# A two-layer diffusion backbone on one core: layer 1's modulation vectors formed on DVE during the dense layer instead of on TensorE in layer 0's scan

## The chip, the cores and the metric

The kernel runs on one core of a Trainium2 chip. The metric is the device time of one execution in microseconds; the median of three runs is given, and one more execution was taken with the hardware profiler.

## The reference, cut to what matters

Two layers work on 256 context tokens and 256 latent tokens of width 1024. Each layer first forms six modulation vectors of 1024 numbers for each of two conditioning vectors, `c` (latent tokens) and `c_ctx` (context tokens):

```python
def modulation(cond, w, b):
    return jnp.split(jax.nn.silu(cond) @ w + b, 6, axis=-1)

h = rms_norm(x, gains[0]) * (1.0 + m[1]) + m[0]        # into the mixers
x = x + m[2] * rms_norm(y, gains[1])                   # behind the output projection
h = rms_norm(x, gains[2]) * (1.0 + m[4]) + m[3]        # into the channel mixer
x = x + m[5] * rms_norm(f, gains[3])
```

The matrix `mod_w[l]` is 1024 x 6144 in float32, 25 MB for a layer. Layer 0 uses all six vectors for both conditioning vectors. Layer 1 drops its context tokens behind the mixers, so for `c_ctx` it uses only the first two. Between the modulated norm and the output projection each layer runs four groups of heads (a bidirectional RWKV-7 recurrence and three kinds of attention). Layer 0's channel mixer is a dense SwiGLU of inner width 2816, layer 1's a mixture of eight experts.

## The kernel before

**Products.** A large product is made of three float32r matmuls (`mm3`): each operand is split into a high and a low part. For weights, a chunk `wr` is loaded by SP's queue (1 MB), ScalarE (ACT) writes the high part `wh`, and VectorE (DVE) the low part `wl` (`wsplit`, lines 189 and 194). Raw chunks and split chunks have three slots each in layer 0's later part.

**Modulation.** `mod_round(l, r)` forms two of the six vectors, a third of a layer's modulation: 16 loads of 128 x 1024 by SP's queue into the four `mw` slots of the pool `mp`, 32 float32 matmuls on TensorE (line 324) with the conditioning vectors `sC` as the stationary operand, padded to 32 columns; then a copy `ms` out of PSUM, four transposes and two additions of the bias into `modT[l]`. The four column pieces of a round go to four groups of 32 rows of one PSUM bank.

**Order.** Instructions are put on the engines by a scheduler that takes what is ready by its own reckoning, in order of priority, which is program order; each engine then runs its queue in that fixed order. A tile whose address was that of an earlier pool waits until the earlier pool is released. Round (0, 0) runs at the start. The rounds (0, 1), (0, 2), (1, 0), (1, 1) and (1, 2) stand in the program behind layer 0's scan, and the scheduler fits their matmuls into what it takes for gaps in the attention, the scan and its readout.

**Layer 0 around the change.** The RWKV recurrence is done as a chunked scan: four chunks of 128 tokens, two directions, a chain of small matmuls with DVE, ACT and POOL between them (`stage_a` to `state`; POOL's subtraction into `R` is line 822, the last matmuls are those of line 875). Then `modS.close()` gives back `mp` and its PSUM bank, and the pools of the output projection are opened, on the same side of SBUF: three raw weight slots first. The readout of the scan (normalisation and gate, lines 979 to 1017) writes `yT[0:2]` and their high and low parts `yh`, `yl`; the other six parts of `yT` come from the attention. The output projection multiplies `yT[2:8]` with weight chunks 0 to 2 and `yT[0:2]` with chunk 3, first for two blocks of 128 tokens, and after a normed addition to the reloaded stream `X` for the other two. `X` is loaded again where `yT` is given back.

**The dense layer.** `ffn` goes through ten chunks of 256 inner columns in five groups of two, and an eleventh by itself. A chunk's gate and up products take all four PSUM banks `mm`; `swiglu` makes `sg` (two slots), `ah` and `al` out of them; behind each second chunk two passes of down products (`ch`) follow, in the four banks `dn`, whose results DVE adds to `fo`. `fg` (two slots) and `xn` (three) are used for norms ahead of and behind this loop. POOL makes the low parts `hl` of the layer's input (line 402).

Of the kernel before, what the change touches and what calls it, by code (L numbers as in the profile page):

```python
# [9 lines left out]
F32 = mybir.dt.float32  # L10
# [4 lines left out]
ALU = mybir.AluOpType  # L15
# [3 lines left out]
D = 1024  # L19
# [133 lines left out]
def kernel(ctx, tc, I, out, dbg=None, stop=None):  # L153
    nc = tc.nc
    dbg = dbg or {}
    V, S_, G, T, SP = nc.vector, nc.scalar, nc.gpsimd, nc.tensor, nc.sync

    cpool = ctx.enter_context(tc.tile_pool(name="cpool", bufs=1))
# [69 lines left out]
    ident = cc("ident")  # L228
    ccol = cpool.tile([128, 16], F32, name="ccol")
    prmt = cpool.tile([128, 2, NPR], F32, name="prmt")  # L230
    prm = [prmt[:, 0], prmt[:, 1]]
# [70 lines left out]
    sC = mp.tile([128, 8, 32], F32, name="sC")  # L302
    V.memset(sC, 0.0)
    sg = cpool.tile([128, 16], F32, name="sg")
    S_.activation(sg, ccol, AF.Tanh, scale=0.5)
    V.tensor_scalar(sg, sg, 0.5, 0.5, op0=ALU.mult, op1=ALU.add)
    for i in range(2):
        V.tensor_tensor(sC[:, :, i], sg[:, 8 * i:8 * i + 8], ccol[:, 8 * i:8 * i + 8], op=ALU.mult)


    modT = [cpool.tile([128, 2, 48], F32, tag="modT", name=f"modT{l}", bufs=2) for l in range(2)]

    def mod_round(l, r):
        pm = mps.tile([128, 512], F32, tag="mod", name="pm", bufs=1)
        for k in range(8):
            for jh in range(2):
                w = mp.tile([128, 1024], F32, tag="mw", name="mw", bufs=4)
                c0 = r * 2048 + jh * 1024
                d = SP.dma_start(out=w, in_=I["mod_w"][l, k * 128:k * 128 + 128, c0:c0 + 1024])
                if l == 0 and r == 0:  # L320
                    WP["first"] = ordered(d)
                for j2 in range(2):
                    j = 2 * jh + j2
                    T.matmul(pm[32 * j:32 * j + 32, :], sC[:, k, :], w[:, j2 * 512:j2 * 512 + 512],  # L324
                             start=(k == 0), stop=(k == 7))
        ms = mp.tile([128, 512], F32, tag="ms", name="ms", bufs=1)
        V.tensor_copy(ms, pm)
        pt = mps.tile([128, 512], F32, tag="mod", name="pt", bufs=1)
        for s in range(4):
            T.transpose(pt[:, s * 128:s * 128 + 128], ms[:, s * 128:s * 128 + 128], ident)  # L330
        pv = pt.rearrange("p (s j c) -> p c j s", s=4, j=4)
        for i in range(2):
            V.tensor_tensor(
                modT[l][:, i, 16 * r:16 * r + 16].rearrange("p (j s) -> p j s", j=4), pv[:, i],
                prm[l][:, 16 * r:16 * r + 16].rearrange("p (j s) -> p j s", j=4), op=ALU.add)

    def scales(l, sec, gi):

# [34 lines left out]
    H = {}  # L373
# [34 lines left out]
    def xn_tile(pool):  # L408
        return pool.tile([128, D + 4], F32, tag="xn", name="xn", bufs=3)
# [161 lines left out]
    def rwkv_mix(l, L, sxa, Sx, rsw, sm, gq, ml, nq, nk_, nv, yT, need):  # L571
# [8 lines left out]
        ps = open_ps(kS, f"pt{l}")  # L580
# [11 lines left out]
        for tb in range(4):  # L592
            p = ps("ra", 1)
# [18 lines left out]
        for q in range(2):  # L612
            p = ps("ra", 1)
# [10 lines left out]
        ps = open_ps(fS, f"rp{l}")  # L624
# [11 lines left out]
        for d in range(2):  # L636
            order = ORD[d]
            first, last = (0, 127) if d == 0 else (127, 0)
            for q in range(2):
# [4 lines left out]
                for a in range(2):  # L644
                    p = ps("rw", 6)
                    for j in range(2):
                        T.matmul(p[:, j * 256:j * 256 + 256],
                                 lw[:, 2 * a + j, d * 256 + q * 128:d * 256 + q * 128 + 128], cc(f"tri{d}"),
                                 start=True, stop=True)
                    pv = p.rearrange("p (j c) -> p j c", j=2)  # L650
# [3 lines left out]
                for n in range(3):  # L654
                    V.tensor_tensor(gg[:, n:n + 1], ee[:, order[n], 128 + last:129 + last],
                                    hm[:, order[n + 1]:order[n + 1] + 1], op=ALU.mult)
                p = ps("rw", 6)
                T.matmul(p, wu[64:128, 512 + d * 256 + q * 128:512 + d * 256 + q * 128 + 128], Sx[6][64:128],
                         start=True, stop=True)
# [27 lines left out]
        for a in range(2):  # L687
            p = ps("rw", 6)
# [259 lines left out]
            while run:  # L948
                run = [g for g in run if next(g, run) is None]
        if l == 0:  # L950
            for m in ((0, 1), (0, 2), (1, 0), (1, 1), (1, 2)):
                mod_round(*m)
        qS.close()
        rBS.close()
# [11 lines left out]
        pm, ht = H["p"], H["t"]  # L966
# [3 lines left out]
        ps = open_ps(oS, f"op{l}")  # L970
# [8 lines left out]
        for q in range(2):  # L979
            p = ps("rw", rwb)  # L980
# [9 lines left out]
        for i in range(4):  # L990
            d, q = i // 2, i % 2
            p = ps("rw", rwb)
# [10 lines left out]
        for i in range(4):  # L1003
            p = ps("rw", rwb)
# [310 lines left out]
    def ffn(l):  # L1315
        sk = ExitStack()
        fp = sk.enter_context(tc.tile_pool(name="ffn", bufs=1))
        ps, pd = H["p"], H["q"]
        fo = fp.tile([128, 4, D], F32, name="fo")
        hh, hl = H["h"]  # L1320
        A2, B2 = scales(l, 4, 2), modT[l][:, :, 24:32]
        hT_half(0, A2, B2, ps, "mm")
        ap_ = sk.enter_context(tc.tile_pool(name="fa", bufs=1))

        def products(g, u, bank, parts):

            if bank is None:
                bank = [[ps("mm", 4) for _ in range(2)] for _ in range(2)]
            for a, b in parts:
                for w, pp in zip((g, u), bank):  # L1330
                    for j in range(2):
                        js = slice(j * 128, j * 128 + 128)
                        for k in range(8):
                            mm3(pp[j][:, a:b], w[0][:, k, js], w[1][:, k, js], hh[:, k, a:b], hl[:, k, a:b],
                                k == 0, k == 7)
            return bank

        def swiglu(bank, ah, al, t, a, b):

            for j, (pg, pu) in enumerate(zip(*bank)):  # L1340
                sg = ap_.tile([128, 512], F32, tag="sg", name="sg", bufs=2)
                S_.activation(sg[:, a:b], pg[:, a:b], AF.Silu)
                V.tensor_tensor(sg[:, a:b], sg[:, a:b], pu[:, a:b], op=ALU.mult)
                S_.activation(ah[:, t + j, a:b], sg[:, a:b], AF.Copy)
                V.tensor_tensor(al[:, t + j, a:b], sg[:, a:b], ah[:, t + j, a:b].bitcast(F32), op=ALU.subtract)


        W = [(wtile(I["fgate"][0], 8), wtile(I["fup"][0], 8))]
        bank = products(*W[0], [[pd("dn", 4) for _ in range(2)] for _ in range(2)], ((0, 256),))
        with tc.high_priority(offset=400):  # L1350
            hT_half(1, A2, B2, ps, "mm")
        products(*W[0], bank, ((256, 512),))
        groups = [(c, c + 2) for c in range(0, 10, 2)]
        for gi, (c0, c1) in enumerate(groups):
            nt = 2 * (c1 - c0)
            ah = ap_.tile([128, 4, 512], F32R, tag="ah", name="ah")
            al = ap_.tile([128, 4, 512], F32R, tag="al", name="al")
            for c in range(c0, c1):
                if c:
                    g, u = wtile(I["fgate"][c], 8), wtile(I["fup"][c], 8)  # L1360
                    bank = products(g, u, None, ((0, 512),))
                swiglu(bank, ah, al, 2 * (c - c0), 0, 512)
            f0 = 2 * c0
            for ch in range(2):
                cs = slice(ch * 512, ch * 512 + 512)
                pts = [pd("dn", 4) for _ in range(4)]
                for t in range(0, nt, 4):
                    m = min(4, nt - t)
                    w = wtile(I["fdown"][ch, :, (f0 + t) * 512:(f0 + t + m) * 512], m)
                    for tb in range(4):  # L1370
                        ts = slice(tb * 128, tb * 128 + 128)
                        for k in range(m):
                            mm3(pts[tb], ah[:, t + k, ts], al[:, t + k, ts], w[0][:, k], w[1][:, k],
                                t + k == 0, t + k == nt - 1)
                for tb in range(4):
                    if gi == 0:
                        act_copy(fo[:, tb, cs], pts[tb])
                    else:
                        V.tensor_tensor(fo[:, tb, cs], fo[:, tb, cs], pts[tb], op=ALU.add)

        gb = [gate_bc(fp, ps, "mm", 4, l, 5, 3, i) for i in (1, 0)]
        ah = ap_.tile([128, 4, 512], F32R, tag="ah", name="ah")
        al = ap_.tile([128, 4, 512], F32R, tag="al", name="al")
        g, u, w = wtile(I["fgate"][10], 8), wtile(I["fup"][10], 8), wtile(I["flast"], 2)
        for a in range(0, 4, 2):
            bank = products(g, u, None, ((a * 128, a * 128 + 256),))
            swiglu(bank, ah, al, 0, a * 128, a * 128 + 256)
            for tb in (a, a + 1):
                ts = slice(tb * 128, tb * 128 + 128)
                for ch in range(2):  # L1390
                    cs = slice(ch * 512, ch * 512 + 512)
                    p = pd("dn", 4)
                    for k in range(2):
                        mm3(p, ah[:, k, ts], al[:, k, ts], w[0][:, k, cs], w[1][:, k, cs], k == 0, k == 1)
                    V.tensor_tensor(fo[:, tb, cs], fo[:, tb, cs], p, op=ALU.add)
            add_normed(H["t"], lambda j, c: fo[:, a + j, c * 512:c * 512 + 512], lambda j: ap_.tile([128, D], F32, tag="fg", name="fg", bufs=2), a,
                       gb[a // 2])
        sk.close()
# [269 lines left out]
```

## Time and profile before

| | before |
|---|---|
| median of 3 runs | 2147.05 us (2142.52 to 2150.84) |
| the profiled execution | 2151.0 us, its span 2149.2 us |
| mean granted TensorE clock | 0.970 |
| TensorE busy (PE) | 2017.5 us, 94% |
| VectorE busy (DVE) | 1348.6 us, 63% |
| ScalarE busy (ACT) | 1118.2 us, 52% |
| GpSimd busy (POOL) | 135.2 us, 6% |

The span is the time from the first to the last instruction of the profiled execution. Times of the trace count from its start. A matmul of float32 operands shows as two records in the trace, one of float32r operands as one. The granted clock is the share of TensorE's full clock (2.4 GHz) that was granted in a stretch. "x" stands ahead of the number of instructions, and an arrow stands ahead of what ended a wait.

### The profile page before, as it was taken

What the parts mean: (1) busy time and instruction counts of PE and PEld (TensorE: products, weight loads), DVE (VectorE), ACT (ScalarE), POOL (GpSimd) and SP (SyncE); (2) the same over time, 40 slices, a digit from 0 to 9 for tenths busy, and PEclk for the clock granted to TensorE, in tenths of its full rate; (3) what the DMA queues carried; (4) which work ended last, traced back from release to release, by engine and by line L of the source; (5) the groups of instructions that cost most, each with busy time, mean ns of one, the idle gap of its engine ahead of it and who ended that gap; (6) DMA issues with size and microseconds to landing.
All of it is one profiled execution on the core that took longest, in us unless ns stands there. A gap on an engine that the chain in (4) does not pass through costs nothing. (4 is left out here: it accounts for less than half of the span.)

```text
span 2149.2 us, 28380 instructions
## 1 busy us (share of the span) xinstructions
PE 2017.5 (94%) x11290; PEld 1547.2 (72%) x11290; DVE 1348.6 (63%) x1934; ACT 1118.2 (52%) x1511; POOL 135.2 (6%) x159
## 2 busy tenths in 40 slices
PE   5999989997999999989997887999999999999997
PEld 2985446743788888879745876878787878787775
DVE  2354475433633333475556556888888888888887
ACT  3344653431532222253464455777676767677774
POOL 1100030120100000011002114000000000000000
PEclk8999999997999999999998998999999999999998
DMA  8411123456222222233001033998899989898993
GB/s 305 149 59 40 59 99 138 139 188 262 79 98 98 98 93 91 85 127 110 1 1 60 2 122 129 354 355 337 330 361 341 345 333 362 340 346 329 351 354 137
DMA packets 65005, 408.62 MB, mean 190 GB/s; under 512 B 7328, under 2 KB 7584, under 8 KB 22880
## 3 DMA queue, kind: packets, MB, share of 16 engines
q1 hardware_dynamic: 62480, 397.69, 49.7%
q0 software_dynamic: 992, 4.92, 0.7%
q10 hardware_dynamic: 1392, 4.11, 0.5%
q8 instruction: 91, 1.49, 0.3%
q14 instruction: 50, 0.41, 0.1%
HBM read 404.60 MB, written 2.10 MB: 189 GB/s over the span
## 5 line engine op out<-in xcount | busy, mean ns | idle before, releaser
L194 DVE TENSOR_TENSOR wl<-wr,wh 128x2048 fp32r<-128x2048 f32 (+3 forms) x395 | 749.6, 1909 | 289.4 <-ACT wh L189 288.4
L189 ACT ACTIVATE wh<-wr 128x2048 fp32r<-128x2048 f32 x327 | 623.3, 1909 | 268.2 <-PE mm L277 91.4
L277 PE MATMUL mm<-wl,gh 128*128 128x512 f32 x704 | 280.4, 398 | 5.5 <-DVE wl L194 5.0
L276 PE MATMUL mm<-wh,gh 128*128 128x512 f32 x704 | 284.5, 404 | 0.4 <-DVE sg L1583 0.4
L278 PE MATMUL mm<-wh,gl 128*128 128x512 f32 x704 | 278.4, 395 | 0.0
L276 PE MATMUL mm<-hh,wh 128*128 128x512 f32 (+1 forms) x544 | 200.9, 369 | 0.8 <-ACT gbc L281 0.8
L278 PE MATMUL mm<-hh,wl 128*128 128x512 f32 (+1 forms) x544 | 200.7, 369 | 0.0
L277 PE MATMUL mm<-hl,wh 128*128 128x512 f32 (+1 forms) x544 | 200.6, 369 | 0.0
L277 PEld LDWEIGHTS mm<-wl,gh 128*128 128x128 f32 x704 | 132.5, 188 | 39.0 <-DVE wl L194 12.1
L278 PEld LDWEIGHTS mm<-wh,gl 128*128 128x128 f32 x704 | 132.3, 188 | 30.6
L276 PEld LDWEIGHTS mm<-wh,gh 128*128 128x128 f32 x704 | 132.3, 188 | 29.2 <-DVE sg L1583 0.5
L278 PE MATMUL yd<-wh,al 128*128 128x512 f32 x352 | 139.7, 397 | 0.0
L277 PE MATMUL yd<-wl,ah 128*128 128x512 f32 x352 | 139.6, 397 | 0.0
L276 PE MATMUL yd<-wh,ah 128*128 128x512 f32 x352 | 130.2, 394 | 0.0
L324 PE MATMUL pm<-mw,sC 128*32 128x512 f32 x384 | 94.4, 677 | 28.3 <-DMA mw<-in_mod_w_dram 21.2
L276 PE MATMUL mm<-wh,hh 128*128 128x256 f32 (+2 forms) x352 | 108.4, 311 | 10.8 <-ACT wh L189 9.4
L276 PEld LDWEIGHTS mm<-hh,wh 128*128 128x128 f32 x544 | 102.6, 189 | 18.2 <-ACT gbc L281 1.0
L278 PEld LDWEIGHTS mm<-hh,wl 128*128 128x128 f32 x544 | 102.5, 188 | 17.3
L277 PEld LDWEIGHTS mm<-hl,wh 128*128 128x128 f32 x544 | 102.6, 189 | 17.2
L278 PE MATMUL mm<-wh,hl 128*128 128x256 f32 (+2 forms) x352 | 108.1, 310 | 1.4 <-POOL hl L402 1.2
L277 PE MATMUL mm<-wl,hh 128*128 128x256 f32 (+2 forms) x352 | 108.3, 309 | 0.0
L281 ACT ACTIVATE ah<-tr 128x256 fp32r<-128x256 f32 x88 | 33.6, 382 | 105.3 <-PE tr L1559 105.3
(415 smaller groups left out, 3249.3 us busy)
## 6 DMA issues: line engine op xcount, KB each, us to landing
wr<-in_mgu_dram SPq DMA_DIRECT2D x176, 1024.0 KB, 5.5
wr<-in_mdown_dram SPq DMA_DIRECT2D x88, 1024.0 KB, 5.0
mw<-in_mod_w_dram SPq DMA_DIRECT2D x96, 512.0 KB, 4.8
wr<-in_w_in_dram SPq DMA_DIRECT2D x20, 1024.0 KB, 4.7
wr<-in_fgate_dram SPq DMA_DIRECT2D x11, 1024.0 KB, 4.8
wr<-in_fup_dram SPq DMA_DIRECT2D x11, 1024.0 KB, 4.7
wr<-in_fdown_dram SPq DMA_DIRECT2D x10, 1024.0 KB, 4.9
wr<-in_w_out_dram SPq DMA_DIRECT2D x9, 1024.0 KB, 4.9
```

Of the source, the lines that this page charges most:

```text
L189: S_.activation(wh, wr, AF.Copy)
L194: WP["eng"].tensor_tensor(wl[:, c], wr[:, c], wh[:, c].bitcast(F32), op=ALU.subtract)
L276: T.matmul(o, lh, rh, start=first, stop=False)
L277: T.matmul(o, lh, rl, start=False, stop=False)
L278: return T.matmul(o, ll, rh, start=False, stop=last)
L281: S_.activation(o, i, AF.Copy)
L324: T.matmul(pm[32 * j:32 * j + 32, :], sC[:, k, :], w[:, j2 * 512:j2 * 512 + 512], start=(k == 0), stop=(k == 7))
```

## The change

Layer 1's three rounds are taken out of the scan. A generator `mod_vector` makes layer 1's modulation in the dense layer instead. For each of the six sections (1024 columns, one vector) it loads eight tiles of 128 x 1024 of `mod_w[1]` by POOL's queue into `fg`, and multiplies each on DVE with a column of 128 numbers of the conditioning vector (one scalar for a partition), adding up in `acc` (an `xn` tile): a `tensor_scalar` for the first tile, a `scalar_tensor_tensor` for the other seven. Sections 0 and 1 do so for both conditioning vectors, the others for `c` alone; the unused part of `modT` is set to zero. At a section's end the sum over partitions is made by matmuls with a matrix `row` that holds one column of ones; then come a copy, four transposes and the addition of the bias as before. The generator is advanced by six steps behind each pass of down products: there are ten passes, a step is one tile, and the end of a section is done in the step behind its eighth tile. The conditioning vectors are kept as `scol` as well.

```diff
+    scol = cpool.tile([128, 2, 8], F32, name="scol")
+    V.tensor_tensor(scol.rearrange("p a b -> p (a b)"), sg, ccol, op=ALU.mult)
     for i in range(2):
-        V.tensor_tensor(sC[:, :, i], sg[:, 8 * i:8 * i + 8], ccol[:, 8 * i:8 * i + 8], op=ALU.mult)
+        V.tensor_copy(sC[:, :, i], scol[:, i])
...
+    def mod_vector(l, row, load, acc_, small, bank):
+        V.memset(row, 0.0)
+        for i in range(2):
+            V.memset(row[:, i, i:i + 1], 1.0)
+        V.memset(modT[l][:, 1, 16:48], 0.0)
+        for sec in range(6):
+            ns = 2 if sec < 2 else 1
+            acc = [acc_() for _ in range(ns)]
+            for k in range(8):
+                w = load()
+                G.dma_start(out=w, in_=I["mod_w"][l, k * 128:k * 128 + 128, sec * 1024:sec * 1024 + 1024])
+                for i in range(ns):
+                    c = scol[:, i, k:k + 1]
+                    if k == 0:
+                        V.tensor_scalar(acc[i], w, c, None, op0=ALU.mult)
+                    else:
+                        V.scalar_tensor_tensor(acc[i], w, c, acc[i], op0=ALU.mult, op1=ALU.add)
+                yield
+            pm = bank()
+            for j in range(2):
+                for i in range(ns):
+                    T.matmul(pm[32 * j:32 * j + 32, :], row[:, i], acc[i][:, j * 512:j * 512 + 512],
+                             start=(i == 0), stop=(i == ns - 1))
+            ms = small()
+            V.tensor_copy(ms[0:64], pm[0:64])
+            pt = bank()
+            for s in range(4):
+                T.transpose(pt[:, s * 64:s * 64 + 64], ms[0:64, s * 128:s * 128 + 128], ident[0:64, 0:64])
+            pv = pt[:, 0:256].rearrange("p (s j c) -> p c j s", s=4, j=2)
+            for i in range(ns):
+                V.tensor_tensor(
+                    modT[l][:, i, 8 * sec:8 * sec + 8].rearrange("p (j s) -> p j s", j=2), pv[:, i],
+                    prm[l][:, 8 * sec:8 * sec + 8].rearrange("p (j s) -> p j s", j=2), op=ALU.add)
...
         if l == 0:
-            for m in ((0, 1), (0, 2), (1, 0), (1, 1), (1, 2)):
+            for m in ((0, 1), (0, 2)):
                 mod_round(*m)
...
+        mods = mod_vector(1, ap_.tile([128, 2, 32], F32, name="row"),
+                          lambda: ap_.tile([128, D], F32, tag="fg", name="fg", bufs=2),
+                          lambda: xn_tile(H["t"])[:, 0:D],
+                          lambda: ap_.tile([128, 512], F32, tag="sg", name="sg", bufs=2), lambda: ps("mm", 4))
         for gi, (c0, c1) in enumerate(groups):
...
                         V.tensor_tensor(fo[:, tb, cs], fo[:, tb, cs], pts[tb], op=ALU.add)
+                for _ in range(6):
+                    next(mods, None)
```

## Rows read from the trace of the kernel before

**Rows 1.** Busy time of each engine by stretch; then granted clock, DMA share, GB/s

```profile
352.50:451.30 98.80, 95.87 (x1200) 73.04 (x1204) 50.43 (x129) 38.56 (x85) 13.21 (x16) 1.00 0.36 124
451.30:494.60 43.30, 38.12 (x137) 9.85 (x136) 14.83 (x19) 15.23 (x26) 7.48 (x6) 0.84 0.66 221
494.60:512.50 17.90, 9.65 (x28) 1.71 (x28) 1.51 (x4) 0.00 (x0) 0.00 (x0) 0.78 0.75 288
...
519.20:543.90 24.70, 24.64 (x96) 19.69 (x97) 10.99 (x11) 7.81 (x9) 0.00 (x0) 0.88 0.53 207
...
605.00:908.00 303.00, 303.00 (x1322) 247.28 (x1321) 108.36 (x121) 76.39 (x71) 0.00 (x0) 1.00 0.27 96
```

**Rows 2.** Timeline behind layer 0's readout: start us, us, engine, line, operation

```profile
494.63 0.69 DVE L1017 TENSOR_TENSOR hl<-yT,hh 128x512 fp32r<-128x512 f32 x1 [0.70 <-ACT hh L281]
...
510.47 0.69 DVE L327 COPY ms<-pm 128x512 f32<-128x512 f32 x1 [15.15 <-PE pm L324]
...
512.40 11.94 SPq L202 DMA_DIRECT2D wr<-in_w_out_dram  x5
...
519.24 1.19 PE L276 MATMUL mm<-wh,hh 128*128 128x512 f32 x2 [6.90 <-ACT wh L189]
```

**Rows 3.** The modulation's matmuls (`pm`) alone, by stretch: PE, PEld, DVE

```profile
352.50:451.30 98.80, 19.91 (x88) 2.83 (x92) 0.68 (x1) 1.00 0.36 124
451.30:494.60 43.30, 19.55 (x84) 3.13 (x84) 0.69 (x1) 0.84 0.66 221
...
416.80:440.80 24.00, 6.20 (x30) 0.88 (x30) 0.68 (x1) 1.00 0.42 140
440.80:451.30 10.50, 2.15 (x8) 0.34 (x12) 0.00 (x0) 1.00 0.37 148
```

**Rows 4.** Timeline of both layers' scans: POOL's `R`, the last output matmuls

```profile
416.77 2.50 POOL L822 TENSOR_TENSOR R<-R,X 128x512 f32<-128x512 f32 x2 [5.53 <-ACT X L281]
...
440.75 2.49 POOL L822 TENSOR_TENSOR R<-R,X 128x512 f32<-128x512 f32 x2 [6.02 <-ACT X L281]
...
450.65 0.65 PE L875 MATMUL b<-Rh,St 64*64 64x128 f32 x8
...
1236.86 2.50 POOL L822 TENSOR_TENSOR R<-R,X 128x512 f32<-128x512 f32 x2 [5.12 <-ACT X L281]
...
1257.69 2.50 POOL L822 TENSOR_TENSOR R<-R,X 128x512 f32<-128x512 f32 x2 [3.84 <-ACT X L281]
...
1266.75 0.65 PE L875 MATMUL b<-Rh,St 64*64 64x128 f32 x8 [0.57 <-DVE Rh L863]
```

**Rows 5.** Timeline of TensorE: the last matmul of layer 1's output projection

```profile
1300.35 0.39 PE L278 MATMUL mm<-wh,hl 128*128 128x512 f32 x1
```

**Rows 6.** Timeline of TensorE: modulation matmuls of two and four pieces, transposes

```profile
417.12 1.97 PE L324 MATMUL pm<-mw,sC 128*32 128x512 f32 x8
...
454.86 1.05 PE L324 MATMUL pm<-mw,sC 128*32 128x512 f32 x4
...
474.88 0.65 PE L330 MATMUL pt<-cst,ms 128*128 128x128 f32 x4 [0.78 <-DVE ms L327]
```

**Rows 7.** Timeline of DVE: two products with a scalar, 128 x 1024

```profile
931.68 2.48 DVE L1303 SCALAR_TENSOR_TENSOR X<-fg,rs_y,X 128x1024 f32<-128x1024 f32 x2
```

**Rows 8.** DMA issues: queue, count, KB each, median us from issue to landing

```profile
mw<-in_mod_w_dram SPq DMA_DIRECT2D x96, 512.0 KB, 4.8
...
X<-in_x_dram ACTq DMA_DIRECT2D x1, 1024.0 KB, 13.9
...
xsave<-X POOLq DMA_DIRECT2D x1, 1024.0 KB, 4.2
X<-xsave POOLq DMA_DIRECT2D x1, 1024.0 KB, 5.7
```

**Rows 9.** Waits from 605 to 908 us: us in total, times, longest

```profile
ACT wh L189 <- PE mm L277: 76.1, 18, 4.6
...
PEld dn L278 <- DVE al L1345: 1.7, 5, 0.3
```

## The prediction

> **What bounds the kernel now.** The busy times by stretch come first [rows 1], since the average over the span (TensorE busy 94%) mixes stages with different limits. In the dense layer's middle, 605 to 908 us, TensorE is busy in all 303 us and DVE in 108: whatever is added to TensorE there is paid in full, and DVE has 195 us to spare. In the last part of layer 0's scan (352.5 to 451.3) TensorE is busy 95.9 of 98.8 us, at the full clock. Behind the scan it is another kernel: 38.1 of 43.3 us busy at a granted clock of 0.84, then 9.7 of 17.9.
>
> The timeline shows why [rows 2]. The readout of the scan is finished with `yl` (the trace calls that tile `hl`) at 495.3. The output projection starts only at 519.2. Between them stand the last modulation matmuls: the copy `ms` at 510.5 ends layer 1's third round but for its transposes, and at 512.4 SP issues the first loads of `w_out`. The reader is to see that these loads wait for nothing of the scan. The tiles `wr` of the new pool lie where the modulation's pool `mp` lay, and `mp` closes with the last round. So 24 us pass with TensorE waiting for weights whose address was held by layer 1's modulation. The projection's first three weight chunks multiply attention outputs (`yT[2]` to `yT[7]`), which were ready long before; they could run inside the readout.
>
> I read the modulation's own matmuls last [rows 3]: layer 1's three rounds take 19.9 us of TensorE between 352.5 and 451.3, and 19.6 us of the 38.1 in the readout.
>
> **What the change removes, and what that is worth.** Removed from the scan are 3 rounds: 48 loads of 512 KB on SP's queue, 96 matmuls, 3 copies and 12 transposes. The round of layer 0 that is left last ends at 352.5, so `mp` is free there, 100 us before the projection wants it, and SP, with no modulation loads ahead of it, can have three chunks of `w_out` in place when the scan ends.
>
> Scan. TensorE looks full, but the chain through DVE, ACT and POOL might set the pace anyhow. Layer 1's scan runs the same steps with no modulation in them [rows 4]. From the third to the fourth `R` subtraction on POOL: 440.75 - 416.77 = 23.98 us in layer 0, 1257.69 - 1236.86 = 20.83 in layer 1. From there to the end of the last output matmuls: 451.30 - 440.75 = 10.55 against 1267.40 - 1257.69 = 9.71. Together 3.99 us less, where layer 0 had 6.20 + 2.15 = 8.35 us of modulation in these two stretches [rows 3]: 0.48 of what is removed comes back. Of 19.9 us I take 9.5. Bounds: 0, if the chain alone counts, and 19.9.
>
> Readout and first half of the projection. Before, from the scan's end to the last matmul of the first four accumulators: 543.9 - 451.3 = 92.6 us. Layer 1 does the same work with its weights loaded early, for 256 columns where layer 0 has 512: 1300.74 - 1267.40 = 33.3 us [rows 4, 5]. The projection of one half is equal in both (96 matmuls, 24.6 us in layer 0 [rows 1]); the readout is twice as wide. Layer 0's readout holds 38.1 - 19.6 = 18.6 us of TensorE without the modulation [rows 1, 3], so half of it, 9.3, comes on top: 42.6 us. Low bound: both brought to the full clock and nothing idle, 18.6 x 0.84 + 24.6 x 0.88 = 37.3. High bound: the readout stays as long as it is (43.3) and only the last quarter of the projection is left behind it (6.2): 49.5.
>
> So 352.5 to 543.9, 191.4 us, becomes 98.8 - 9.5 + 42.6 = 131.9: **59.5 us less** (43.1 to 75.2). What is late next is the reload of `X`: it is issued when `yT` is free and took 13.9 us to land [rows 8]. It would land about 4 us after the last matmul of the first half; the second half of the projection (another 96 matmuls, 22 us) covers it, so it costs nothing. Without that cover it would be 4 us.
>
> **What the change adds, in the dense layer.** TensorE: 16 matmuls and 24 transposes. The two column halves of a section run side by side, as the modulation's do: 1.05 us for such a pair [rows 6]. Sections 2 to 5: 4 x 1.05. Sections 0 and 1 have two accumulating matmuls for each half, which I price by the slower row, 1.97 each. Transposes: 0.65 us for four [rows 6], six times. 4.2 + 3.9 + 3.9 = 12.0 us, all paid, for TensorE never idles there.
>
> DVE: 64 products of 128x1024. A `scalar_tensor_tensor` of that size took 2.48/2 = 1.24 us [rows 7]; all at that price: 79 us. With the 108 that DVE has, 187 of 303: it doesn't become the bound. Nothing of it is in TensorE's way directly. The weight splits have cover: ACT's split waits for TensorE to release a slot 18 times, 76.1 us in all [rows 9], so the splits run a whole tile ahead. Without that cover each would cost up to 1.24 us. Thin cover is at the ends of the chunks, where the `sg`, `ah`, `al` chain ends just ahead of the down matmuls: five times TensorE already waits for `al`, 1.7 us in all [rows 9]. A product already running delays it by up to 1.24 us; with half of that at each of ten chunks, 6.2 us.
>
> Loads: the 48 move from SP's queue to POOL's, two buffers of `fg`. SP's queue loses what stood before `w_out`; on POOL's the `hl` subtractions of the dense layer's input stand before or between them, and the first two loads find empty buffers and hold nobody. On SP such a load took 4.8 us to land; POOL's 1024 KB took 4.2 and 5.7 [rows 8]. Take 4.9. Two buffers then allow some 7 us for a pair, 170 us for 48: it fits in 303. DMA is busy 0.27 there [rows 1]. But DVE takes its instructions in order, and a product whose load is late holds `sg` and `al` behind it; TensorE takes its own in order too, and a reduction whose sum is late holds the products. Nothing in the trace of before shows either. Bound from below: nothing; from above: half a landing, 2.5 us, at each of ten chunks, 25 us. I keep the 6.2 us, nearer the low end, since the splits show how far ahead the work there runs. Sum: **18.2 us more** (12 to 37). The extra copy at the very start is one DVE operation of some 0.2 us.
>
> One rule speaks against POOL's queue. The Trainium skill, page "SBUF — State Buffer", section "Who interferes with whom", says that DVE in a two-port mode and GpSimd lock each other out, and that a transfer issued from GpSimd then seems stalled, because its descriptors can't be written. By that rule the eight first products of the sections (`tensor_scalar`) could hold a load's start and the others, with two tensor inputs, could not; the sum would stay as it is. The trace has no transfer from POOL beside such a DVE load, so it neither agrees nor differs.
>
> **Rivals.** (a) The scan and the readout are held by their own chains, not by the modulation: both high bounds, 43.1 - 18.2 = 25 us won, 2122. For it: the DVE and ACT waits inside the readout; against it: layer 1's 33.3 us. (b) The reductions wait: six sections, each with a late sum of one landing and one product, 4.9 + 1.2, is 37 us more, 4 won, 2143. Against it: the sums have some 50 us each to be formed. (c) Slower: DVE's queue is held at its head by late loads when a chunk ends. Ten chunks times a full landing, 49 us, in place of the 6.2 leaves 41.3 - 43 = 2 us lost, 2149; it decides from 4.7 us a chunk on, and becomes a loss of 0.5% only near 5.8, which is longer than these loads take, so loads must also become slower. If all loads were held up by DVE as that page of the Trainium skill describes for its two-port modes, that is how it would look. (d) The change does not free the space: `w_out` still waits for the scan's own tiles and is loaded at its end. Then a landing and a split, 4.9 + 1.9, come on top: 2113. (e) All of the 19.9 us and the full-clock readout: 75.2 - 12 = 63 won, 2084.
>
> **How the numbers follow.** 59.5 - 18.2 = 41.3 us won. The profiled execution took 2151.0 us (span 2149.2), 3.95 above the median of the three runs; 2151.0 - 41.3 = 2109.7, and on the median's footing 2105.8: **2106 us**. Chances: the forecast, with (d) in it, 0.64 (2090 to 2120); (a) 0.20; (b) 0.08; (c) 0.04; (e) 0.04. Range: (e)'s 2084 at the low end, and at the high end (a) with some of (b), 2130; left out are most of (b) and (c), the tail of (e). A time within 0.5%, 10.7 us, is about what can't be told from no change. Faster by more: 0.64 + 0.20 + 0.04 and a little of (b), 0.89; the rest of (b), 0.07; slower 0.04.
>
> **What would show it.** Right: `w_out` issued on SP near 353 to 360; the projection's first matmul within some 6 us of the scan's end, and no gap of 24 us; a granted clock of 1 in the readout; the scan's last two stretches near 21 and 10 us; DVE near 187 us in the dense layer, whose middle is 12 to 20 us longer. Wrong: DVE idle with a load as releaser just ahead of `sg` or `al`, or TensorE waiting for `acc`, by tens of us; or a projection that still starts late.

## The result and the profile after

The changed kernel takes 2124.64 us, median of 4 runs (2119.65 to 2125.24), beside 2147.99 (2142.52 to 2150.84) of the kernel before: a ratio of 0.9889, 95% interval 0.9864 to 0.9914. It is faster by 23 us, where 41 were forecast. The time lies inside the range (2084 to 2130), but above the 2090 to 2120 that the forecast's own case was to give. The two profiled spans, 2149.2 and 2122.0 us, differ by 27.2 us, and that is shared out here.

Busy times by stretch, as in [rows 1], the first from the scan's first `TMI` copy on POOL to its last output matmul, the second to the end of the projection's first half, the third to the start of POOL's first `hl` subtraction behind the dense layer (it makes layer 1's input; E1's expectation calls it the layer's last); then two stretches inside the third:

```profile
298.50:443.54 145.04, 127.31 (x1452) 98.77 (x1450) 90.47 (x194) 62.19 (x144) 31.58 (x34) 0.96 0.13 48
443.54:483.81 40.27, 37.10 (x146) 23.49 (x146) 26.34 (x29) 24.00 (x37) 7.46 (x6) 1.00 0.59 223
483.81:926.39 442.58, 417.09 (x1994) 339.79 (x1994) 256.45 (x348) 131.89 (x160) 32.50 (x53) 0.97 0.42 143
624.00:644.00 20.00, 13.78 (x55) 10.46 (x53) 9.98 (x9) 3.67 (x4) 2.65 (x5) 0.91 0.75 249
644.00:664.00 20.00, 17.20 (x68) 12.37 (x69) 12.36 (x17) 2.54 (x2) 1.05 (x2) 0.84 0.35 111
```

| stretch | before | after | |
|---|---|---|---|
| up to the scan's first `TMI` copy | 293.8 | 298.5 | 4.7 more |
| scan, to its last output matmul | 157.5 | 145.0 | 12.5 less |
| readout and first half of the projection | 92.9 | 40.3 | 52.7 less |
| from there to POOL's first `hl` subtraction behind the dense layer | 408.0 | 442.6 | 34.6 more |
| the rest | 1196.9 | 1195.6 | 1.3 less |

In the kernel before, the last matmul of the projection's first half starts at 543.86 and ends at 544.25. The forecast counted to its start (92.6, and 408.4 in E1's expectation), this table to its end, as in the other traces.

The gain came as forecast: the readout runs at a granted clock of 1.00 instead of 0.84. The price in the dense layer is 34.6 us instead of 18. Two views tell where. The waits of this stretch (what waited for what: us in total, times, longest), and below them the like one of the kernel before:

```profile
DVE xn L357 <- DMA fg<-in_mod_w_dram: 45.3, 22, 5.1
...
PE dn L276 <- ACT ah L1382: 11.7, 4, 6.0
PE mm L368 <- DVE sg L365: 5.8, 2, 4.4
```

```profile
PE dn L276 <- ACT ah L1344: 0.2, 1, 0.2
```

Before, the down matmuls waited 0.2 us in all for `ah`; now they wait 11.7 us, four times, and the reductions' transposes (L368) 5.8 us for their copy. The worst place is the end of the fourth weight chunk. The timeline there:

```profile
618.63 0.58 ACT L1380 ACTIVATE sg<-mm 128x512 f32<-128x512 f32 x1
...
623.13 0.53 POOL L351 DMA_DIRECT2D fg<-in_mod_w_dram  x1 [3.53 <-DVE xn L357]
...
624.66 0.58 ACT L1380 ACTIVATE sg<-mm 128x512 f32<-128x512 f32 x1
...
628.08 0.39 PE L278 MATMUL mm<-hh,wl 128*128 128x512 f32 x1
...
630.62 2.61 DVE L357 SCALAR_TENSOR_TENSOR xn<-fg,scol,xn 128x1024 f32<-128x1024 f32 x2 [5.09 <-DMA fg<-in_mod_w_dram]
...
633.14 2.35 DVE L194 TENSOR_TENSOR wl<-wr,wh 128x1024 fp32r<-128x1024 f32 x2
...
633.52 0.39 PE L278 MATMUL mm<-hh,wl 128*128 128x512 f32 x1
...
636.10 1.28 DVE L357 SCALAR_TENSOR_TENSOR xn<-fg,scol,xn 128x1024 f32<-128x1024 f32 x1 [0.61 <-DMA fg<-in_mod_w_dram]
...
638.66 1.28 DVE L357 SCALAR_TENSOR_TENSOR xn<-fg,scol,xn 128x1024 f32<-128x1024 f32 x1 [1.27 <-DMA fg<-in_mod_w_dram]
639.86 0.68 DVE L1381 TENSOR_TENSOR sg<-sg,mm 128x512 f32<-128x512 f32 x1
...
640.57 0.63 ACT L1382 ACTIVATE ah<-sg 128x512 fp32r<-128x512 f32 x1 [15.33 <-DVE sg L1381]
...
641.26 0.79 PE L276 MATMUL dn<-wh,ah 128*128 128x512 f32 x1 [5.97 <-ACT ah L1382]
...
641.85 0.63 PE L277 MATMUL dn<-wl,ah 128*128 128x512 f32 x1
...
645.41 0.68 DVE L1381 TENSOR_TENSOR sg<-sg,mm 128x512 f32<-128x512 f32 x1
...
646.80 0.79 PE L276 MATMUL dn<-wh,ah 128*128 128x512 f32 x1 [3.05 <-ACT ah L1382]
```

A chunk has two halves, each with a Silu of its gate product on ACT and a multiplication by its up product on DVE (L1381). Each product takes 24 matmuls, and the up products come last: the first is complete at 628.47 and the second at 633.91, behind the last `mm` matmul. The gates' Silus were done at 619.21 and 625.24. DVE multiplies at 639.86 and 645.41, 11.4 and 11.5 us behind the up products; in the kernel before, 0.04 us behind them at each chunk's end. What stood ahead of the first multiplication in DVE's queue, from 625.5 on: waits for loads of 5.09 + 0.61 + 1.27 = 7.0 us, four products (5.2) and two splits (2.4). TensorE waits 5.97 us and then 3.05, and its matmuls, 0.39 us each ahead of the first wait, take 0.63 behind it: the granted clock is 0.91 and 0.84 in these two stretches of 20 us, so 1.2 GHz in parts of them.

### The profile page after: what moved, and what is told of

Same layout as the page of the kernel before. It is cut to its first block, busy times and chain, and to the rows that moved or that the text cites. A ratio compares the mean times of both kernels' runs of the same rounds, so it can differ in the third digit from the quotient of the medians.

```text
span 2122.0 us, 28210 instructions
## 1 busy us (share of the span) xinstructions
PE 1986.3 (94%) x11142; PEld 1543.1 (73%) x11142; DVE 1424.1 (67%) x2008; ACT 1116.1 (53%) x1511; POOL 160.6 (8%) x207
## 5 line engine op out<-in xcount | busy, mean ns | idle before, releaser
L357 DVE SCALAR_TENSOR_TENSOR xn<-fg,scol,xn 128x1024 f32<-128x1024 f32 x56 | 71.9, 1299 | 45.7 <-DMA fg<-in_mod_w_dram 45.3
```

Source lines behind the costliest of these rows:

```text
L357: V.scalar_tensor_tensor(acc[i], w, c, acc[i], op0=ALU.mult, op1=ALU.add)
```

## The experiments

Every experiment starts from the changed kernel. "Dense stretch" is the third stretch above, found by the same instructions in each trace. How well two traces agree is told by E4 and E10, which are one kernel: 424.1 and 426.1 us, so differences under some 2 us say nothing.

**E1: no modulation for layer 1.**

```diff
     def mod_vector(l, row, load, acc_, small, bank):
-        V.memset(row, 0.0)
...
+        V.tensor_copy(modT[l], modT[0])
+        return
```

> Layer 1's modulation is left out altogether (no loads, no products, no reductions; layer 1 gets a copy of layer 0's modulation, so its routing and all that follows it mean nothing for the time). The stretch from the last matmul of the projection's first half to the layer's last subtraction on POOL took 408.4 us before the change and 442.6 after it. Every theory expects 405 to 411 here: the 34 us are all of the moved work. If it were 420 or more, part of the 34 us would come from something else that the change moved (the order of the splits, the clock).

The window row of the dense stretch:

```profile
480.98:887.52 406.54, 397.51 (x1938) 332.23 (x1938) 178.13 (x263) 132.04 (x160) 6.02 (x4) 1.00 0.27 94
```

406.5 us, 2083.7 us in all. Without the moved work the dense stretch is no longer than before (408.0), so that work is the whole of its loss, and 442.6 - 406.5 = 36 us is the most that a cheaper way to do it could still win.

**E2: the loads alone.**

```diff
                 G.dma_start(out=w, in_=I["mod_w"][l, ...])
-                for i in range(ns):
...
                 yield
-            pm = bank()
...
```

> The 48 loads stay on POOL's queue with two buffers; their products and the reductions are left out (layer 1 gets a copy of layer 0's modulation). Theory A (late loads hold DVE's queue at its head, and the splits, the sg/ah/al chain and the reductions' copy wait behind them): the loads alone cost nothing, 406 to 412 us. Theory B (the products' own time on DVE is what is in the way): the same. Theory C (the loads take the DMA engines or the memory from the weights): 420 us or more, with TensorE or ACT waiting for weights' loads.

Its window row, and the largest wait of PE:

```profile
479.72:890.74 411.02, 398.53 (x1938) 333.58 (x1938) 178.74 (x263) 132.28 (x160) 30.55 (x52) 0.99 0.45 155
```

```profile
PE dn L277 <- POOL hl L415: 5.8, 2, 4.5
```

411.0 us, 4.5 more than with no loads, and no wait for a weight's load among TensorE's: theory C falls. What there is, PE's waits for `hl`, is POOL: the loads stand in its queue ahead of the dense input's `hl` subtractions, and in this kernel the loads wait only for each other. In the changed kernel that wait is 1.8 us, in E1 2.6.

**E3: products and reductions, one load.**

```diff
+        w = None
...
-                w = load()
-                G.dma_start(...)
+                if w is None:
+                    w = load()
+                    G.dma_start(...)
```

> One load instead of 48: all 64 products take the same tile, so no product waits for a load; the reductions stay (layer 1's modulation is another one, so what follows the dense layer means nothing for the time). Theory A: 408.4 + 11 us of TensorE work + some 0 to 8 us of delays at chunk ends = 420 to 427 us. Theory B: 438 to 446 us, as with the loads. Theory C: like A, but then the loads alone are dear.

```profile
478.33:901.51 423.18, 410.76 (x1994) 334.61 (x1994) 256.22 (x348) 132.15 (x160) 8.17 (x5) 1.00 0.26 92
```

423.2 us: the 64 products and the reductions cost 423.2 - 406.5 = 16.6 us. TensorE is busy 13.3 us longer than in E1 (410.76 against 397.51), and 3.4 us more of it is idle. DVE has the same 256 us of work as in the changed kernel, so theory B falls: a product in the way costs little if its load is there. The loads' lateness costs 442.6 - 423.2 = 19.4 us: TensorE idles 13.1 us longer (25.5 against 12.4), and is busy 6.3 us longer with the same 1994 matmuls, at the lower granted clock (0.97 against 1.00). The planner puts DVE's queue in another order here, too; whether that matters is taken up behind E9.

**E4: four tiles for the loads**, two of `fg` and the two that the gates use at the layer's end.

```diff
+        n4 = iter(range(48))
...
-                          lambda: ap_.tile([128, D], F32, tag="fg", name="fg", bufs=2),
+                          lambda: (fp.tile([128, D], F32, tag="gbc", name="gbc", bufs=2) if next(n4) % 2 else
+                                   ap_.tile([128, D], F32, tag="fg", name="fg", bufs=2)),
```

> Four tiles take the loads instead of two (every second load goes into the tiles that the gates use at the end of the layer). Theory A: loads come earlier, DVE's waits for them fall from 45 us to under 20, and 6 to 14 of the 34 us come back: 428 to 437 us. Theory B: 442 us, as after the change. Theory C: 442 us or more.

Its window row, then its largest wait for loads and the largest of PE, then the first multiplication at the fourth chunk's end from the timeline:

```profile
482.28:906.38 424.10, 410.99 (x1994) 334.88 (x1994) 256.01 (x348) 132.06 (x160) 32.51 (x52) 1.00 0.44 150
```

```profile
DVE xn L357 <- DMA gbc<-in_mod_w_dram: 7.9, 4, 4.8
PE mm L368 <- DVE sg L365: 4.0, 2, 2.6
```

```profile
625.09 0.69 DVE L1381 TENSOR_TENSOR sg<-sg,mm 128x512 f32<-128x512 f32 x1 [1.36 <-PE mm L278]
```

424.1 us, better than theory A's numbers: all of the loads' price is gone, with the loads themselves still there. DVE waits 9 us for loads instead of 47, PE's waits for the reductions' copy, its largest, come to 4.0 us, and the granted clock is 1.00. At the fourth chunk's end DVE now waits for the up product, and not the other way round.

**E5: two tiles, the loads on SP's queue.**

```diff
-                G.dma_start(out=w, in_=I["mod_w"][l, ...])
+                SP.dma_start(out=w, in_=I["mod_w"][l, ...])
```

> The 48 loads are issued on SP's queue, between the weights' loads, with two tiles as in the changed kernel. If the number of tiles is what makes the loads late, they are late here too, and SP's queue, which waits for a free tile in order, holds the weights' loads behind it: the dense stretch 440 to 470 us (442.6 after the change, 424.1 with four tiles). If POOL's queue is what makes them late (its loads held up while DVE works), two tiles on SP do as well as four on POOL: 422 to 428 us.

```profile
480.20:907.84 427.64, 412.15 (x1995) 335.68 (x1994) 255.62 (x348) 132.57 (x160) 7.23 (x5) 1.00 0.44 148
```

```profile
DVE xn L357 <- DMA fg<-in_mod_w_dram: 40.2, 19, 5.2
...
PE dn L276 <- ACT ah L1382: 2.1, 2, 1.9
```

The timeline at the fourth chunk's end:

```profile
623.92 0.39 PE L278 MATMUL mm<-hh,wl 128*128 128x512 f32 x1
...
626.84 0.68 DVE L1381 TENSOR_TENSOR sg<-sg,mm 128x512 f32<-128x512 f32 x1
...
629.36 0.39 PE L278 MATMUL mm<-hh,wl 128*128 128x512 f32 x1
...
631.54 1.28 DVE L357 SCALAR_TENSOR_TENSOR xn<-fg,scol,xn 128x1024 f32<-128x1024 f32 x1 [2.63 <-DMA fg<-in_mod_w_dram]
632.75 0.68 DVE L1381 TENSOR_TENSOR sg<-sg,mm 128x512 f32<-128x512 f32 x1
...
634.14 0.65 PE L276 MATMUL dn<-wh,ah 128*128 128x512 f32 x1 [1.87 <-ACT ah L1382]
634.59 0.63 PE L277 MATMUL dn<-wl,ah 128*128 128x512 f32 x1
```

427.6 us, which the first reading did not expect, and it corrects theory A as I had put it. The time is that of the second reading, but not for its reason: the loads come no earlier, for DVE waits 40.2 us for them, nearly the 45.3 of the changed kernel. Yet this costs 4.5 us (427.6 - 423.2) instead of 19.4. The sum of DVE's waits is not the price. A late load costs where the multiplication of a chunk's end stands behind it: at the fourth chunk's end the two run 2.5 and 3.0 us behind their up products here (624.31 and 629.75), the first with no load wait in between and the second behind one of 2.63, and 11.4 and 11.5 us in the changed kernel.

**E6: the same two tiles on POOL, the steps spread** over each pair of weight chunks.

```diff
                 swiglu(bank, ah, al, 2 * (c - c0), 0, 512)
+                for _ in range(3):
+                    next(mods, None)
...
-                for _ in range(6):
+                for _ in range(2 + ch):
                     next(mods, None)
```

> Two tiles on POOL's queue as in the changed kernel, but the steps are handed out in twos and threes, four times for each pair of weight chunks, instead of six behind each half of the down matmuls. If the loads are late because they come in bursts, the even spacing brings back as much as four tiles did: 422 to 430 us. If two tiles are too few at any spacing, because the planner packs the products anyway, 436 to 446 us.

```profile
480.35:936.05 455.70, 419.64 (x1994) 340.91 (x1994) 256.39 (x348) 132.23 (x160) 32.50 (x52) 0.97 0.41 139
```

```profile
DVE xn L357 <- DMA fg<-in_mod_w_dram: 47.7, 21, 5.2
PE dn L276 <- ACT ah L1382: 15.0, 5, 4.4
PE mm L368 <- DVE sg L365: 6.9, 3, 4.7
PE dn L276 <- ACT wh L189: 5.4, 1, 5.4
```

455.7 us, 13 worse than the changed kernel and outside both expectations. DVE's waits are about the same again (47.7 us); TensorE's are longer.

**E9: spread steps with four tiles** (the diffs of E4 and E6).

> The even spacing of the steps, which made the dense stretch 455.7 us with two tiles, now with four tiles. If its loss was late loads standing in DVE's queue ahead of a chunk's last products (the same cause as in the changed kernel, at other places), four tiles bring it to 423 to 430 us. If it was the place of the products themselves, loads or not, it stays at 440 us or more.

```profile
479.91:903.06 423.15, 410.12 (x1994) 335.14 (x1994) 256.22 (x348) 132.44 (x160) 32.89 (x52) 1.00 0.44 150
```

423.2 us, beside 424.1 of E4: these two ways to hand out the steps make no difference once the loads are early. With two tiles, the steps handed out as here cost 32.5 us more.

The planner orders DVE's queue anew in every one of these kernels, so its order is a rival to the early loads. The first multiplication at the fourth chunk's end, read in the same way in each trace, speaks against it:

| | changed | E3 | E4 | E5 | E6 | E9 |
|---|---|---|---|---|---|---|
| us behind its up product | 11.4 | 0.0 | 0.0 | 2.5 | 11.6 | 0.0 |
| products ahead of it in DVE's queue, of 64 | 39 | 40 | 40 | 36 | 39 | 40 |

As many products stand ahead of it where it is in time as where it is 11 us late. So it is late by their loads, not by their number. Their exact places do differ (between it and the multiplication before it stand 7 in the changed kernel, 5 in E4 and E9), so some part of the 19.4 us may still be the order.

**E7: four tiles (the diff of E4), and `w_out` loaded early.**

```diff
-        open_w(XS["w"], f"wb{l}", 3, 3)
+        if l == 0:
+            for i in range(3):
+                open_raw(XS["w"], f"wo{i}", 1)
+        open_w(XS["w"], f"wb{l}", 3 if l else 0, 3)
```

> Four tiles for the loads as before, and the three tiles that take the projection's first weights are opened as three pools instead of one, so that two of them no longer wait for the scan's tiles. SP issues two of these loads near 352 us instead of at the scan's end. If the late weights set the 10.2 to 11.6 us from the scan's end to the projection's first matmul, it becomes 3 to 6 us, and the first half ends 33 to 37 us behind the scan instead of 40.3 to 41.6. If the readout's own chain sets that end, the first matmul is earlier but the end stays at 39 to 42. The dense stretch stays at 422 to 426 us.

In the changed kernel SP issues `w_out` at the scan's end (443.54), against the forecast of 353 to 360, and the projection starts 10 us behind it. The timeline of the changed kernel:

```profile
443.62 14.23 SPq L202 DMA_DIRECT2D wr<-in_w_out_dram  x5
```

```profile
453.75 0.80 PE L276 MATMUL mm<-wh,hh 128*128 128x512 f32 x1
```

The timeline of E7, whose scan ends at 440.80:

```profile
354.16 87.05 SPq L202 DMA_DIRECT2D wr<-in_w_out_dram  x3
...
440.88 0.33 SPq L202 DMA_DIRECT2D wr<-in_w_out_dram  x1
```

```profile
448.50 0.59 ACT L1038 ACTIVATE tmp<-rw 128x512 f32<-128x512 f32 x1
448.97 3.71 ACT L189 ACTIVATE wh<-wr 128x2048 fp32r<-128x2048 f32 x2
```

```profile
452.39 0.79 PE L276 MATMUL mm<-wh,hh 128*128 128x512 f32 x1
```

The first row merges three loads: two are issued at 354, and the third, in the second row by itself, still at the scan's end. Nothing is won, and the projection's start does not move, which neither reading expected: it starts 11.6 us behind the scan, and its first half ends 41.4 us behind it (E4: 11.6 and 41.4). ACT's split of the weights comes only at 448.97, behind the readout's own instructions in ACT's queue (in E4 at 449.00). The late load was there, and it was covered. What an earlier split would win is not shown, for ACT's order stayed as it was.

**E8: four tiles, the partition sums as columns.**

```diff
-            T.matmul(pm[32 * j:32 * j + 32, :], row[:, i], acc[i][:, j * 512:j * 512 + 512], ...)
-            ... copy, four transposes
+            T.matmul(p[:, 8 * i + j:8 * i + j + 1], acc[i][:, j * 128:j * 128 + 128], cc("ones")[:, 0:1], ...)
```

> Four tiles, and the partition sums taken another way: the sum tile is the stationary operand and a column of ones moves, so that a section's sums come out as columns, by 8 or 16 matmuls of one column, without the copy and the transposes (64 matmuls in place of 32 + 24). The reductions cost 11 us of TensorE and 4.0 us of waits for their copy with four tiles. A one-column matmul is bounded by its weight load of 128x128, some 0.1 to 0.2 us: 6 to 13 us in all, without the waits: the dense stretch 415 to 423 us instead of 424.1. If the one-column matmuls are dearer than 0.25 us each, 425 us or more.

422.6 us in the dense stretch and 2107.8 in all, beside 424.1 and 2106.9 of E4: no difference that can be told. The weight loads of the one-column matmuls took 0.19 us each, TensorE is busy 1.6 us longer, and the waits for the copy are gone.

**E10, E11, E12: timed**, five rounds each beside the kernel before (2148.6 us, 9 runs, 2145.29 to 2153.83): E4's kernel, E8's kernel, and E8's with the loads on SP.

> Four tiles, timed. One look gave 2106.9 us beside 2149.9 of before: ratio 0.979 to 0.982, below the changed kernel's 0.9889 by about 0.9%.

> Four tiles and the column sums, timed. The dense stretch was 1.5 us shorter than with four tiles alone, the whole 0.9 us longer in one look: the same as four tiles alone within 0.2%, ratio 0.979 to 0.982.

> Four tiles, the loads on SP's queue, and the column sums. If POOL's queue costs anything of its own (DVE holding up its descriptors, or the hl subtractions behind waiting loads), the dense stretch falls below 420 us and the ratio to 0.977 or less. If the number of tiles was the whole matter, 421 to 425 us and a ratio of 0.979 to 0.982.

| | median us | ratio | 95% interval | dense stretch |
|---|---|---|---|---|
| E10: four tiles | 2103.87 | 0.9794 | 0.9780 to 0.9808 | 426.1 |
| E11: and column sums | 2105.76 | 0.9803 | 0.9788 to 0.9819 | 424.2 |
| E12: and the loads on SP | 2107.10 | 0.9810 | 0.9794 to 0.9825 | 424.2 |

All three came as expected of them. Four tiles beat the changed kernel, whose interval (0.9864 to 0.9914) lies wholly above. The column sums and SP's queue add nothing to that.

## Why the prediction was right, and where it was off

**The sum.** The total is inside the range in part by luck. The measured 2124.6 us stands beside the 2122 of rival (a), whose mechanism is not what happened. The range reached up to 2130 because of (a), not because of what the dense layer cost. The scan and the readout gave 5.7 us more than forecast (3.0 and 2.7), the dense layer took 16.4 more, and the 4.7 of the start are scatter.

**The scan.** Forecast 9.5 us less, measured 12.5 over the whole scan. The two steps that I took from layer 1 came out almost to the hundredth: from the third to the fourth `R` on POOL 23.98 us before [rows 4], 20.84 now, and from there to the last output matmul 10.55 before, 9.71 now (443.54 - 433.83). The 3.0 us beyond the forecast lie ahead of the third `R`: there I had carried over the share of 0.48, 5.5 of 11.6 us, and 8.5 came back. The timeline:

```profile
412.99 2.50 POOL L860 TENSOR_TENSOR R<-R,X 128x512 f32<-128x512 f32 x2 [4.61 <-ACT X L281]
...
433.83 2.50 POOL L860 TENSOR_TENSOR R<-R,X 128x512 f32<-128x512 f32 x2 [3.85 <-ACT X L281]
```

**Readout and projection.** Forecast 42.6 us, measured 40.3, at a granted clock of 1.00. The statement that `w_out` is issued near 353 was wrong and rival (d) was right about the space: the loads wait for the scan's tiles. But the 6.8 us that I gave (d) weren't lost: E7 took the wait away for two of the three loads and won nothing. What I had priced by layer 1's whole readout held the readout's own chain already.

**The start.** 4.7 us more in the profiled run, forecast at one DVE operation of 0.2. The changed kernel and the experiments issue the same instructions in the same order up to there (in E1 and E2 a small DVE operation stands elsewhere), and their thirteen `TMI` copies start at 291.0 to 298.5 us, 294.2 in the mean, beside 293.8 before; E4 and E10, one kernel, are 4.5 apart. This is scatter between executions, and the changed kernel's profile was the latest of all.

**The dense layer.** Forecast 18.2, measured 34.6. DVE doesn't become the bound, as forecast: 256 us of 443. Two of its three terms came out near: TensorE's work 12.0 against 13.3, the products' delay 6.2 against 3.4 (E3). The third failed, and it is the mis-sized one: for the loads I had put 0 between bounds of 0 and 25 ("nearer the low end, since the splits show how far ahead the work there runs"); it measured 19.4 (442.6 - 423.2; four tiles gave it back). The argument looked at the splits, which do run a tile ahead, and not at the multiplication L1381 at a chunk's end, which can't: it stands behind whatever products the planner put ahead of it, and with two tiles each pair of these needs a fresh landing. At the fourth chunk's end it ran 11.4 us behind its up product, and TensorE waited. My average was right (48 loads fit well into the stretch) and of no use, because the products stand in runs of up to seven. I had no term for the clock; 6.3 of the 19.4 us are that. Together the measured terms are 36.1 us, counted from E1, whose stretch is 1.5 us shorter than before.

**The rivals.** (c)'s mechanism is what happened, at 19.4 us in place of its 49: not at ten chunk ends, but at a few, and the loads did not become slower (median landing 4.6 us). (b): the reductions never waited for the sums, only for the copy behind them, 5.8 us in place of 37. (a) had the right time and is excluded by its mechanism: the scan came back by 12.5 us, where (a) gave it nothing, and the readout runs at a clock of 1.00. (e) is excluded by the scan, which gave back 12.5 of the 19.9 us, and by the dense layer.

**The loads of POOL and DVE.** POOL's issuing instruction took 0.53 us at its median and 0.58 at the longest of 48, and the loads landed in 4.6 us beside the products and 5.3 us without any (E2). With four tiles the queue makes no difference (E11 and E12, 424.2 both). The Trainium skill, page "SBUF — State Buffer", section "Who interferes with whom", lets a POOL-issued transfer stall beside DVE's two-port operations, for want of port time to write its descriptors, and names transfers on the hardware's path (HWDGE) as the cure. These runs show nothing of it. With two tiles SP did better than POOL (E5), but DVE's order differs between the two kernels as well, so that difference has two possible causes; which of them it is was not settled.

## What to carry to other kernels

Work moved to an engine with idle time is not free because its share fits: look at what stands behind it in that engine's queue, and give its loads enough tiles that those ahead of a deadline land in time (here four did what two didn't; three were not tried). The sum of an engine's waits for loads does not price them (40.2, 45.3 and 47.7 us of them cost 4.5, 19.4 and 32.5 us here); look at what the bound engine waits for, and at its clock. A wait that the trace shows is worth removing only if nothing else ends just behind it; an early load of `w_out` won nothing, because ACT's split of it came no earlier.

## What the hardware showed that was not expected

TensorE's lower clock made a third of the loads' price (6.3 of 19.4 us). At the fourth chunk's end TensorE idled 5.97 us and, 2.5 us after that wait ended, 3.05 us more; its matmuls of 128x512 took 0.63 us instead of 0.39 behind both waits. Even a wait of 1.87 us in E5 was followed by matmuls of 0.63 us. In the kernel before, the dense layer's middle ran at 1.00 throughout [rows 1], so nothing of this could be read there.
